# Index-add on one core: staged batches spread through the copies, their stores moved behind the last copy

## The chip, the cores and the metric

The kernel runs on one core of a Trainium2 chip. The metric is the device time of one execution in microseconds (us); the kernel before was run three times, with a median of 92.13 us. "The span" is the time from the first to the last of the program's own instructions in one profiled execution.

## The reference

For each of 32 batches, 128 rows of 256 float32 numbers are added to rows of a 512-row table. An index may occur several times in one batch, and then all of its rows are added.

```python
batch, seq, dim = 32, 512, 256
num_updates = 128
result = x.copy()
for b in range(batch):
    for i in range(num_updates):
        result[b, indices[b, i]] += source[b, i]
```

One batch of x, and so of the output, is 512 KB. One batch of source is 128 KB, and the sources of four batches are loaded together as one group of 512 KB.

## The kernel before, in words

Two ways lead to a finished batch.

**A direct batch** (0 to 25, `N_DIRECT = 26`). SP copies the whole batch from x to the output, DRAM to DRAM, in pieces of 4096 elements at most (`copy`, L97). GpSimd (POOL) gathers the 128 rows that the indices name into `got` with an indirect DMA (L189). TensorE multiplies a mask of equal indices (`same`) with the source rows, so that each row of the result holds the sum over all updates with that index (L266), and VectorE (DVE) adds this to the gathered rows, two batches at a time (L278). Then POOL scatters the rows over the copy with another indirect DMA (L346). A row whose index occurred earlier in the batch gets a place outside the table (`to_i`, L250) and isn't written. A scatter may start only when the copy of its batch has landed, since it overwrites rows of it, and when its sum is ready.

**A staged batch** (26 to 31). SP loads the whole batch into SBUF (`load_x`, L110). VectorE makes a one-hot matrix of the indices (L287), TensorE spreads the source rows over the 512 rows with it in two halves (L302), VectorE adds the halves to the loaded batch (L312), and ACT stores the finished batch (L323). There is no gather and no scatter.

**The order of the work.** Each engine runs its instructions in the order in which they are written.

- SP issues the index load, then source groups 0 and 1, then rounds of one source group, one load of a staged batch and two copies, with the source groups in the order 6, 7, 2, 3, 4, 5. After six rounds copies 10 to 25 remain and are issued one after the other. All this goes through one queue, which the profile calls q1. [...]
- ACT issues the six stores of the staged batches, each as soon as VectorE has finished the batch. They go through a queue of their own, q10.
- POOL issues 26 gathers, then 26 scatters in the order of the batches, then runs one `drain` (L354). Its transfers go through q0.
- TensorE and VectorE take the groups of four batches in order: for each group the mask of the next one (TensorE L206, VectorE L221, L233, L241, L250), then the sums of this one, then one staged batch.
- At the end SP waits for all six stores and then for all 26 scatters (L357), and the engines meet at the end of the program (L92). `tile_critical(no_gpsimd_drain=True)` is in both kernels, so the drain of L354 is the only one written.

Of the kernel before, what the change touches and what calls it, by code (L numbers as in the profile page):

```python
# [7 lines left out]
P = 128  # L8


GB = 4
COPY_DESC = 4096
N_DIRECT = 26


@with_exitstack
def kernel(
# [11 lines left out]
    nc = tc.nc  # L29

    B, S, D = x.shape
    _, NU = indices.shape
    CH = S // P
    assert NU == P and S % P == 0 and B % GB == 0 and N_DIRECT % 2 == 0
    NG = B // GB
    NGD = (N_DIRECT + GB - 1) // GB
    STAGED = list(range(N_DIRECT, B))

    f32 = mybir.dt.float32
    i32 = mybir.dt.int32  # L40
# [3 lines left out]
    x_rows = x.rearrange("b s d -> (b s) d")  # L44
    out_rows = out.rearrange("b s d -> (b s) d")

    sb = ctx.enter_context(tc.tile_pool(name="sb", bufs=1))
# [12 lines left out]
    row_i = sb.tile([P, B], i32)  # L60
    dup = sb.tile([P, B], f32)
    to_i = sb.tile([P, B], i32)
    src = [sb.tile([P, GB, D], f32, name=f"src{g}") for g in range(NG)]
    got = [sb.tile([P, 2, D], f32, name=f"got{h}") for h in range(N_DIRECT // 2)]
    same = [sb.tile([P, GB, P], f32, name=f"same{g}") for g in range(NGD)]
    earlier = [sb.tile([P, GB, P], f32, name=f"earlier{k}") for k in range(2)]
    staged = {b: sb.tile([P, CH, D], f32, name=f"staged{b}") for b in STAGED}
    onehot = {b: sb.tile([P, CH, P], f32, name=f"onehot{b}") for b in STAGED}
    N_ADD, N_SP = 3, 2
    idx_ps = pp.tile([P, B], f32, space=PSUM)  # L70
    bc = [pp.tile([P, GB, P], f32, space=PSUM, name=f"bc{k}") for k in range(2)]
    add = [pp.tile([P, 2, D], f32, space=PSUM, name=f"add{k}") for k in range(N_ADD)]
# [1 line left out]

    s_idx = tc.alloc_semaphore("s_idx")
    s_src = [tc.alloc_semaphore(f"s_src{g}") for g in range(NG)]
    s_copy = [tc.alloc_semaphore(f"s_copy{b}") for b in range(N_DIRECT)]
    s_got = [tc.alloc_semaphore(f"s_got{b}") for b in range(N_DIRECT)]
    s_in = {b: tc.alloc_semaphore(f"s_in{b}") for b in STAGED}
    s_out = tc.alloc_semaphore("s_out")  # L80
    s_store = tc.alloc_semaphore("s_store")
    sems = {n: tc.alloc_semaphore(f"s_{n}") for n in ("pool", "dve", "pe")}
    done = dict.fromkeys(sems, 0)

    def mark(name, ins):
        ins.then_inc(sems[name], 1)
        done[name] += 1
        return done[name]

    V, T, G, A = nc.vector, nc.tensor, nc.gpsimd, nc.scalar  # L90

    with tc.tile_critical(no_gpsimd_drain=True):  # L92

# [2 lines left out]
        def copy(b):  # L96
            nc.sync.dma_start(  # L97
                out=out[b].rearrange("(p c) d -> p (c d)", p=P),
                in_=x[b].rearrange("(p c) d -> p (c d)", p=P),
                max_dma_last_dim=COPY_DESC,  # L100
            ).then_inc(s_copy[b], 16)

        def load_src(g):
            nc.sync.dma_start(  # L104
                out=src[g][:, :, :],
                in_=source[g * GB : (g + 1) * GB].rearrange("e u d -> u e d"),
            ).then_inc(s_src[g], 16)

        def load_x(b):
            nc.sync.dma_start(  # L110
                out=staged[b][:, :, :], in_=x[b].rearrange("(j c) d -> j c d", c=CH)
            ).then_inc(s_in[b], 16)

        load_src(0)
        load_src(1)
        copies, sources, loads = list(range(N_DIRECT)), list(range(2, NG)), list(STAGED)
        sources = sources[-2:] + sources[:-2]
        while copies or sources or loads:
            if sources:
                load_src(sources.pop(0))  # L120
            if loads:
                load_x(loads.pop(0))
            for b in copies[:2]:
                copy(copies.pop(0))


        m = mark("pool", G.memset(ident[:, :], 0.0))  # L127
# [4 lines left out]
                out=ident[:, :], in_=ident[:, :], compare_op=Alu.not_equal, fill=1.0,  # L132
# [10 lines left out]
                out=place[:, :, :], pattern=[[1, CH], [CH, P]], base=0, channel_multiplier=0  # L143
# [8 lines left out]
                out=before[:, :, :], in_=before[:, :, :], compare_op=Alu.is_gt, fill=0.0,  # L152
# [8 lines left out]
        k = mark(  # L161
            "dve",
            V.tensor_copy(  # L163
                out=idx_bt[:, :],
                in_=idx_raw[:, :].rearrange("b (u w) -> b u w", w=2)[:, :, 0],
            ),
        )
        T.wait_ge(sems["pool"], k_const)
        T.wait_ge(sems["dve"], k)
        k = mark("pe", T.transpose(out=idx_ps[:, :], in_=idx_bt[:, :], identity=ident[:, :]))  # L170
        V.wait_ge(sems["pe"], k)
        k_rows = mark(
            "dve",
            V.tensor_tensor(out=row_i[:, :], in0=idx_ps[:, :], in1=base_f[:, :], op=Alu.add),
        )
# [7 lines left out]
        m = mark("dve", V.tensor_copy(out=place_f[:, :, :], in_=place[:, :, :]))  # L183
        V.wait_ge(sems["dve"], m)


        G.wait_ge(sems["dve"], k_rows)
        for b in range(N_DIRECT):
            G.indirect_dma_start(  # L189
                out=got[b // 2][:, b % 2, :],  # L190
                out_offset=None,
                in_=x_rows,
                in_offset=bass.IndirectOffsetOnAxis(ap=row_i[:, b : b + 1], axis=0),
            ).then_inc(s_got[b], 16)

        k_bc, k_same, k_to, k_sum, k_hot, k_spread = {}, {}, {}, {}, {}, {}

        def pe_broadcast(g):

            if g >= 2:  # L200
                T.wait_ge(sems["dve"], k_same[g - 2])
            for e in range(GB):
                b = g * GB + e
                k_bc[g] = mark(
                    "pe",
                    T.matmul(  # L206
                        out=bc[g % 2][:, e, :],
                        lhsT=ident[:, b : b + 1].to_broadcast([B, P]),
                        rhs=idx_bt[:, :],
                        start=True,  # L210
                        stop=True,
                    ),
                )
# [42 lines left out]
        def sums(g):  # L256

            T.wait_ge(s_src[g], 16)
            T.wait_ge(sems["dve"], k_same[g])
            for b in range(g * GB, min((g + 1) * GB, N_DIRECT)):  # L260
                h = b // 2
                if b % 2 == 0 and h >= N_ADD:
                    T.wait_ge(sems["dve"], k_sum[h - N_ADD])
                k = mark(
                    "pe",
                    T.matmul(  # L266
                        out=add[h % N_ADD][:, b % 2, :], lhsT=same[g][:, b % GB, :],
                        rhs=src[g][:, b % GB, :], start=True, stop=True,
                    ),
                )  # L270
                if b % 2 == 0:
                    continue
                V.wait_ge(sems["pe"], k)
                V.wait_ge(s_got[b - 1], 16)
                V.wait_ge(s_got[b], 16)
                k_sum[h] = mark(
                    "dve",
                    V.tensor_tensor(  # L278
                        out=got[h][:, :, :], in0=got[h][:, :, :],
                        in1=add[h % N_ADD][:, :, :], op=Alu.add,  # L280
                    ),
                )

        def dve_onehot(b):
            k_hot[b] = mark(
                "dve",
                V.tensor_scalar(  # L287
                    out=onehot[b][:, :, :], in0=place_f[:, :, :],
                    scalar1=idx_f[:, b : b + 1], scalar2=None, op0=Alu.is_equal,
                ),  # L290
            )
# [26 lines left out]
        def staged_batch(b):  # L318
            dve_onehot(b)
            pe_spread(b, 0)  # L320
            k = pe_spread(b, 1)
            A.wait_ge(sems["dve"], k)
            A.dma_start(  # L323
                out=out[b].rearrange("(j c) d -> j c d", c=CH), in_=staged[b][:, :, :]
            ).then_inc(s_store, 16)

        pe_broadcast(0)
        dve_masks(0)
        pe_broadcast(1)
        todo = list(STAGED)  # L330
        for g in range(NGD):
            if g + 1 < NGD:
                dve_masks(g + 1)
            if g + 2 < NGD:
                pe_broadcast(g + 2)
            sums(g)
            if todo:
                staged_batch(todo.pop(0))
        for b in todo:
            staged_batch(b)  # L340


        for b in range(N_DIRECT):
            G.wait_ge(s_copy[b], 16)
            G.wait_ge(sems["dve"], max(k_sum[b // 2], k_to[b // GB]))  # L345
            G.indirect_dma_start(  # L346
                out=out_rows,
                out_offset=bass.IndirectOffsetOnAxis(ap=to_i[:, b : b + 1], axis=0),
                in_=got[b // 2][:, b % 2, :],
                in_offset=None,  # L350
                bounds_check=B * S - 1,
                oob_is_err=False,
            ).then_inc(s_out, 16)
        G.drain()  # L354

        nc.sync.wait_ge(s_store, 16 * len(STAGED))
        nc.sync.wait_ge(s_out, 16 * N_DIRECT)  # L357
# [30 lines left out]
```

## Time and profile before

| what | value |
|---|---|
| three runs, median (lowest to highest) | 92.13 us (90.91 to 94.13) |
| the profiled execution's own time | 91.28 us |
| its span | 89.6 us |
| PE, DVE and POOL busy | 42.9, 36.2 and 53.6 us |
| bytes moved by the DMA engines | 30.61 MB |
| HBM read and written | 24.41 and 20.19 MB |

The page gives the span in 40 equal slices; a digit is the busy share of a slice in tenths. The DMA row is the mean over the core's 16 DMA engines, and the GB/s row is what they moved. A DRAM-to-DRAM copy counts once in GB/s but is read from HBM and written to it. A view of windows gives the same figures for any stretch of the span; there the share can pass 1, because transfers on one engine overlap a little. Times in the views are us from the start of the span.

### The profile page before, as it was taken

The page shows a single profiled execution, that of the slowest core. Times are in us where ns is not written, and L with a number is a line of the kernel's source. Part 1 is how long each engine was busy: PE and PEld are TensorE (multiplying, and loading weights), DVE is VectorE, ACT ScalarE, POOL GpSimd, SP SyncE. Part 2 cuts the span into 40 slices and gives each one's busy share as a digit, 9 for nine tenths or more (in the row PEclk, how much of TensorE's full clock was granted, in tenths as well). Part 3 has the DMA queues.
Part 4 walks back from the last instruction along what each step waited for, and adds up shares of the span by engine and source line. Part 5 has one row for each costly group of instructions (what it writes and reads, how often), then busy time and mean ns, then how long its engine had stood idle before and what let it go on. Part 6 is the DMA issues. An engine that isn't in the chain of part 4 may idle for free.

```text
span 89.6 us, 646 instructions
## 1 busy us (share of the span) xinstructions
PE 42.9 (48%) x157; PEld 32.8 (37%) x157; DVE 36.2 (40%) x65; POOL 53.6 (60%) x62
## 2 busy tenths in 40 slices
PE   0699950999299292949965358693000000000000
PEld 0698710776286271727745144581000000000000
DVE  2659416069669668342694964335000000000000
POOL 5778777877778777877786400446643448575400
PEclk9999999579999999555999985569655555555555
DMA  0899999999999999999999999999999999983200
GB/s 8 268 284 336 404 399 412 411 412 400 405 417 400 409 412 414 412 405 402 405 394 419 416 414 422 351 346 299 406 415 378 280 345 392 397 352 139 86 0 0
DMA packets 12243, 30.61 MB, mean 342 GB/s; under 512 B 1584, under 2 KB 5721, under 8 KB 12240
## 3 DMA queue, kind: packets, MB, share of 16 engines
q1 hardware_dynamic: 8880, 21.01, 63.2%
q0 software_dynamic: 2496, 6.42, 18.7%
q10 hardware_dynamic: 864, 3.15, 8.8%
q8 instruction: 1, 0.02, 0.1%
q14 instruction: 2, 0.02, 0.0%
HBM read 24.41 MB, written 20.19 MB: 498 GB/s over the span
## 4 chain that ended last, share of the span: by engine, by line
SPq 55%; DMA 24%; issue 8%; POOL 4%; POOLq 2%
DMA out_dram<-in_x_dram 24%; SPq L97 21%; SPq L104 17%; SPq L110 17%; POOL out_dram L346 4%; POOLq L354 1%; SPq L94 0%; POOLq L345 0%; POOLq L346 0%; SPq L383 0%; SPq L92 0%
## 5 line engine op out<-in xcount | busy, mean ns | idle before, releaser
L346 POOL DMA_INDIRECT out_dram<-got,to_i x26 | 26.0, 1000 | 21.1 <-DMA out_dram<-in_x_dram 7.8
L189 POOL DMA_INDIRECT got<-in_x_dram,row_i x26 | 25.3, 972 | 8.1 <-issue 7.0
L302 PE MATMUL spread<-src,onehot 128*128 128x256 f32 x48 | 16.4, 501 | 11.1 <-issue 7.5
L266 PE MATMUL add<-src,same 128*128 128x256 f32 x52 | 17.1, 484 | 4.1 <-DMA src<-in_source_dram 4.1
L302 PEld LDWEIGHTS spread<-src,onehot 128*128 128x128 f32 x48 | 11.9, 260 | 16.3 <-issue 14.2
L266 PEld LDWEIGHTS add<-src,same 128*128 128x128 f32 x52 | 11.7, 235 | 7.3 <-DMA src<-in_source_dram 4.7
L312 DVE TENSOR_TENSOR staged<-staged,spread 128x512 f32<-128x512 f32 x12 | 8.3, 688 | 13.1 <-PE spread L302 13.1
L278 DVE TENSOR_TENSOR got<-got,add 128x512 f32<-128x512 f32 x13 | 8.7, 685 | 8.4 <-PE add L266 4.5
L206 PE MATMUL bc<-idx_bt,ident 32*128 32x128 f32 x56 | 10.1, 342 | 0.0
L206 PEld LDWEIGHTS bc<-idx_bt,ident 32*128 32x128 f32 x56 | 9.1, 246 | 1.4 <-issue 0.7
L221 DVE TENSOR_TENSOR same<-bc,idx_f 128x512 f32<-128x512 f32 x7 | 4.8, 684 | 1.1 <-PE bc L206 1.1
L233 DVE TENSOR_TENSOR earlier<-same,before 128x512 f32<-128x512 f32 x7 | 4.8, 692 | 0.3
L241 DVE TENSOR_REDUCE dup<-earlier 128x4 f32<-128x512 f32 x7 | 4.8, 686 | 0.2
L287 DVE TENSOR_SCALAR onehot<-place_f,idx_f 128x512 f32<-128x512 f32 x6 | 2.9, 479 | 0.0
L170 PE MATMUL idx_ps<-ident,idx_bt 32*128 32x32 f32 x1 | 0.3, 279 | 3.1 <-DVE idx_bt L163 3.1
L159 DVE CAST base_f<-base 128x32 f32<-128x32 int32 x1 | 1.0, 993 | 1.7 <-POOL base L137 1.7
L170 PEld LDWEIGHTS idx_ps<-ident,idx_bt 32*128 32x128 f32 x1 | 0.2, 178 | 3.1 <-POOL before L147 3.1
L250 DVE SCALAR_TENSOR_TENSOR to_i<-dup,row_f 128x4 int32<-128x4 f32 x7 | 1.1, 162 | 0.2
L151 POOL TENSOR_SCALAR_AFFINE_SELECT before<-before 128x512 f32<-128x512 f32 x1 | 0.7, 708 | 0.1
L142 POOL IOTA place<- 128x512 int32 x1 | 0.6, 553 | 0.0
L147 POOL MEMSET before<- 128x512 f32 x1 | 0.5, 514 | 0.0
L127 POOL MEMSET ident<- 32x32 f32 x1 | 0.1, 114 | 0.5 <-SPq L92 0.5
(11 smaller groups left out, 2.0 us busy)
## 6 DMA issues: line engine op xcount, KB each, us to landing
out_dram<-in_x_dram SPq DMA_DIRECT2D x26, 512.0 KB, 17.9
src<-in_source_dram SPq DMA_DIRECT2D x8, 512.0 KB, 12.9
staged<-in_x_dram SPq DMA_DIRECT2D x6, 512.0 KB, 15.7
out_dram<-staged ACTq DMA_DIRECT2D x6, 512.0 KB
got<-in_x_dram,row_i POOLq DMA_INDIRECT x26, 5.9
out_dram<-got,to_i POOLq DMA_INDIRECT x26, 6.3
idx_raw<-in_indices_dram SPq DMA_DIRECT2D x1, 32.0 KB, 1.7
```

The source lines that it names most:

```text
L97: nc.sync.dma_start(out=out[b].rearrange("(p c) d -> p (c d)", p=P), in_=x[b].rearrange("(p c) d -> p (c d)", p=P), max_dma_last_dim=COPY_ ...
L104: nc.sync.dma_start(out=src[g][:, :, :], in_=source[g * GB : (g + 1) * GB].rearrange("e u d -> u e d"),).then_inc(s_src[g], 16)
L110: nc.sync.dma_start(out=staged[b][:, :, :], in_=x[b].rearrange("(j c) d -> j c d", c=CH)).then_inc(s_in[b], 16)
L189: G.indirect_dma_start(out=got[b // 2][:, b % 2, :], out_offset=None, in_=x_rows, in_offset=bass.IndirectOffsetOnAxis(ap=row_i[:, b : b + ...
L206: T.matmul(out=bc[g % 2][:, e, :], lhsT=ident[:, b : b + 1].to_broadcast([B, P]), rhs=idx_bt[:, :], start=True, stop=True,),
L221: V.tensor_tensor(out=same[g][:, :, :], in0=bc[g % 2][:, :, :], in1=idx_f[:, gs].unsqueeze(2).to_broadcast([P, GB, P]), op=Alu.is_equal,),
L233: V.tensor_tensor(out=earlier[g % 2][:, :, :], in0=same[g][:, :, :], in1=before[:, :, :], op=Alu.mult,),
L266: T.matmul(out=add[h % N_ADD][:, b % 2, :], lhsT=same[g][:, b % GB, :], rhs=src[g][:, b % GB, :], start=True, stop=True,),
L278: V.tensor_tensor(out=got[h][:, :, :], in0=got[h][:, :, :], in1=add[h % N_ADD][:, :, :], op=Alu.add,),
L302: T.matmul(out=spread[n % N_SP][:, c, :], lhsT=onehot[b][:, 2 * half + c, :], rhs=src[b // GB][:, b % GB, :], start=True, stop=True,),
L312: V.tensor_tensor(out=rows, in0=rows, in1=spread[n % N_SP][:, :, :], op=Alu.add),
L346: G.indirect_dma_start(out=out_rows, out_offset=bass.IndirectOffsetOnAxis(ap=to_i[:, b : b + 1], axis=0), in_=got[b // 2][:, b % 2, :], in ...
```

## The change

Three things change; what is computed doesn't.

- **Which batches are staged.** Six batches are staged as before, but now 7, 11, 15, 19, 23 and 27 in place of 26 to 31. Twenty-six are direct, as before; the direct batches are paired in their own order for `got` and for the sums, so that batch 6 shares a pair with batch 8.
- **The order of SP's queue.** Source groups are issued in the order 0 to 7, each two groups ahead, and each staged load two copies after its group. The six stores are no longer ACT's. SP issues them behind the last copy, each behind a wait for VectorE's last addition to that batch.
- **The order on VectorE and TensorE.** The staged batch of a group is computed behind the sums of the next group. A mask is made for the eighth group too, since batches 28 to 31 are direct now.

The gathers, the scatters and the drain keep their code and their number; their batch numbers follow the list of direct batches.

```diff
-N_DIRECT = 26
+STAGED = (7, 11, 15, 19, 23, 27)
...
-        copies, sources, loads = list(range(N_DIRECT)), list(range(2, NG)), list(STAGED)
-        sources = sources[-2:] + sources[:-2]
-        while copies or sources or loads:
-            if sources:
-                load_src(sources.pop(0))
-            if loads:
-                load_x(loads.pop(0))
-            for b in copies[:2]:
-                copy(copies.pop(0))
+        for g in range(NG):
+            if g + 2 < NG:
+                load_src(g + 2)
+            for b in range(g * GB, (g + 1) * GB):
+                if b in DIRECT:
+                    copy(b)
+                if b % GB == 1 and g * GB - 1 in STAGED:
+                    load_x(g * GB - 1)
...
-            A.wait_ge(sems["dve"], k)
-            A.dma_start(
-                out=out[b].rearrange("(j c) d -> j c d", c=CH), in_=staged[b][:, :, :]
-            ).then_inc(s_store, 16)
+            k_staged[b] = k
...
-        for g in range(NGD):
-            if g + 1 < NGD:
+        for g in range(NG):
+            if g + 1 < NG:
                 dve_masks(g + 1)
-            if g + 2 < NGD:
+            if g + 2 < NG:
                 pe_broadcast(g + 2)
             sums(g)
-            if todo:
-                staged_batch(todo.pop(0))
-        for b in todo:
-            staged_batch(b)
+            if g * GB - 1 in STAGED:
+                staged_batch(g * GB - 1)
...
         G.drain()
+
+
+        for b in STAGED:
+            nc.sync.wait_ge(sems["dve"], k_staged[b])
+            nc.sync.dma_start(
+                out=out[b].rearrange("(j c) d -> j c d", c=CH), in_=staged[b][:, :, :]
+            ).then_inc(s_store, 16)
```

SP's queue near its end, before. `src5` is a source group, `staged31` the load of a staged batch, and `out` from `x` a copy; x16 stands for sixteen of them in a row.

```order
L97 DMA out_0_dram<-in_x_dram 128x1024 x2
L104 DMA src4_78<-in_source_dram 128x4x256
L110 DMA staged30_108<-in_x_dram 128x1024
L97 DMA out_0_dram<-in_x_dram 128x1024 x2
L104 DMA src5_79<-in_source_dram 128x4x256
L110 DMA staged31_109<-in_x_dram 128x1024
L97 DMA out_0_dram<-in_x_dram 128x1024 x16
```

The same place now:

```order
L111 DMA staged19_108<-in_x_dram 128x1024
L98 DMA out_0_dram<-in_x_dram 128x1024 x3
L111 DMA staged23_109<-in_x_dram 128x1024
L98 DMA out_0_dram<-in_x_dram 128x1024 x3
L111 DMA staged27_110<-in_x_dram 128x1024
L98 DMA out_0_dram<-in_x_dram 128x1024 x2
L363 DMA out_0_dram<-staged7_105 128x1024
L363 DMA out_0_dram<-staged11_106 128x1024
L363 DMA out_0_dram<-staged15_107 128x1024
L363 DMA out_0_dram<-staged19_108 128x1024
L363 DMA out_0_dram<-staged23_109 128x1024
L363 DMA out_0_dram<-staged27_110 128x1024
```

The sixteen copies in a row have become runs of at most four, with loads between them, and the last rows of the queue are now the six stores; before, the last row was a copy.

VectorE's order around a staged batch late in the program, before:

```order
L250 SCALAR_TENSOR_TENSOR to_i_73<-dup_72,row_f_70 128x4
L278 TENSOR_TENSOR got10_92<-got10_92,add1_120 128x512
L278 TENSOR_TENSOR got11_93<-got11_93,add2_121 128x512
L287 TENSOR_SCALAR onehot31_115<-place_f_67,idx_f_68 128x512
L312 TENSOR_TENSOR staged31_109<-staged31_109,spread0_122 128x512
L312 TENSOR_TENSOR staged31_109<-staged31_109,spread1_123 128x512
L278 TENSOR_TENSOR got12_94<-got12_94,add0_119 128x512
```

And now:

```order
L272 TENSOR_TENSOR got9_91<-got9_91,add0_120 128x512
L272 TENSOR_TENSOR got10_92<-got10_92,add1_121 128x512
L281 TENSOR_SCALAR onehot23_115<-place_f_67,idx_f_68 128x512
L306 TENSOR_TENSOR staged23_109<-staged23_109,spread0_123 128x512
L306 TENSOR_TENSOR staged23_109<-staged23_109,spread1_124 128x512
L272 TENSOR_TENSOR got11_93<-got11_93,add2_122 128x512
L272 TENSOR_TENSOR got12_94<-got12_94,add0_120 128x512
L281 TENSOR_SCALAR onehot27_116<-place_f_67,idx_f_68 128x512
L306 TENSOR_TENSOR staged27_110<-staged27_110,spread0_123 128x512
L306 TENSOR_TENSOR staged27_110<-staged27_110,spread1_124 128x512
```

The last sums of direct batches (`got11`, `got12`) stand behind the update of batch 23 now, and the last thing that VectorE does is the update of batch 27, for which SP's last store waits.

More of the change, by code (lines that the diff above doesn't have):

```diff
@@ L33 @@
     CH = S // P
-    assert NU == P and S % P == 0 and B % GB == 0 and N_DIRECT % 2 == 0
+    assert NU == P and S % P == 0 and B % GB == 0
     NG = B // GB
-    NGD = (N_DIRECT + GB - 1) // GB
-    STAGED = list(range(N_DIRECT, B))
+    DIRECT = [b for b in range(B) if b not in STAGED]
+    N_DIRECT = len(DIRECT)
+    assert N_DIRECT % 2 == 0
     f32 = mybir.dt.float32
@@ L64 @@
     got = [sb.tile([P, 2, D], f32, name=f"got{h}") for h in range(N_DIRECT // 2)]
-    same = [sb.tile([P, GB, P], f32, name=f"same{g}") for g in range(NGD)]
+    same = [sb.tile([P, GB, P], f32, name=f"same{g}") for g in range(NG)]
     earlier = [sb.tile([P, GB, P], f32, name=f"earlier{k}") for k in range(2)]
@@ L76 @@
     s_src = [tc.alloc_semaphore(f"s_src{g}") for g in range(NG)]
-    s_copy = [tc.alloc_semaphore(f"s_copy{b}") for b in range(N_DIRECT)]
-    s_got = [tc.alloc_semaphore(f"s_got{b}") for b in range(N_DIRECT)]
+    s_copy = {b: tc.alloc_semaphore(f"s_copy{b}") for b in DIRECT}
+    s_got = {b: tc.alloc_semaphore(f"s_got{b}") for b in DIRECT}
     s_in = {b: tc.alloc_semaphore(f"s_in{b}") for b in STAGED}
@@ L88, in mark @@
         return done[name]
-    V, T, G, A = nc.vector, nc.tensor, nc.gpsimd, nc.scalar
+    V, T, G = nc.vector, nc.tensor, nc.gpsimd
     with tc.tile_critical(no_gpsimd_drain=True):
@@ L184 @@
         V.wait_ge(sems["dve"], m)
[L187 to L194, printed above, removed]
         k_bc, k_same, k_to, k_sum, k_hot, k_spread = {}, {}, {}, {}, {}, {}
+        k_staged = {}
         def pe_broadcast(g):
@@ L259, in sums @@
             T.wait_ge(sems["dve"], k_same[g])
-            for b in range(g * GB, min((g + 1) * GB, N_DIRECT)):
-                h = b // 2
-                if b % 2 == 0 and h >= N_ADD:
+            for b in range(g * GB, (g + 1) * GB):
+                if b in STAGED:
+                    continue
+                n = DIRECT.index(b)
+                h = n // 2
+                if n % 2 == 0 and h >= N_ADD:
                     T.wait_ge(sems["dve"], k_sum[h - N_ADD])
@@ L266, in sums @@
                     T.matmul(
-                        out=add[h % N_ADD][:, b % 2, :], lhsT=same[g][:, b % GB, :],
+                        out=add[h % N_ADD][:, n % 2, :], lhsT=same[g][:, b % GB, :],
                         rhs=src[g][:, b % GB, :], start=True, stop=True,
@@ L270, in sums @@
                 )
-                if b % 2 == 0:
+                if n % 2 == 0:
                     continue
                 V.wait_ge(sems["pe"], k)
-                V.wait_ge(s_got[b - 1], 16)
+                V.wait_ge(s_got[DIRECT[n - 1]], 16)
                 V.wait_ge(s_got[b], 16)
@@ L329, with gather, scatter @@
         pe_broadcast(1)
-        todo = list(STAGED)
-        for g in range(NGD):
-            if g + 1 < NGD:
+        for g in range(NG):
+            if g + 1 < NG:
                 dve_masks(g + 1)
-            if g + 2 < NGD:
+            if g + 2 < NG:
                 pe_broadcast(g + 2)
             sums(g)
-            if todo:
-                staged_batch(todo.pop(0))
-        for b in todo:
-            staged_batch(b)
-        for b in range(N_DIRECT):
+            if g * GB - 1 in STAGED:
+                staged_batch(g * GB - 1)
+        def gather(n):
+            b = DIRECT[n]
+            G.indirect_dma_start(
+                out=got[n // 2][:, n % 2, :],
+                out_offset=None,
+                in_=x_rows,
+                in_offset=bass.IndirectOffsetOnAxis(ap=row_i[:, b : b + 1], axis=0),
+            ).then_inc(s_got[b], 16)
+        def scatter(n):
+            b = DIRECT[n]
             G.wait_ge(s_copy[b], 16)
-            G.wait_ge(sems["dve"], max(k_sum[b // 2], k_to[b // GB]))
+            G.wait_ge(sems["dve"], max(k_sum[n // 2], k_to[b // GB]))
             G.indirect_dma_start(
@@ L348 @@
                 out_offset=bass.IndirectOffsetOnAxis(ap=to_i[:, b : b + 1], axis=0),
-                in_=got[b // 2][:, b % 2, :],
+                in_=got[n // 2][:, n % 2, :],
                 in_offset=None,
@@ L353 @@
             ).then_inc(s_out, 16)
-        G.drain()
+        G.wait_ge(sems["dve"], k_rows)
+        for n in range(N_DIRECT):
+            gather(n)
+        for n in range(N_DIRECT):
+            scatter(n)
+        G.drain()
+        for b in STAGED:
[3 more added lines that the diff above has]
+            ).then_inc(s_store, 16)
         nc.sync.wait_ge(s_store, 16 * len(STAGED))
```

## The prediction

> **What bounds the kernel now.** I read the page's slices first, then its queues, and then the last ten microseconds row by row.
>
> ```profile
> DMA  0899999999999999999999999999999999983200
> q1 hardware_dynamic: 8880, 21.01, 63.2%
> q0 software_dynamic: 2496, 6.42, 18.7%
> q10 hardware_dynamic: 864, 3.15, 8.8%
> ```
>
> The DMA engines are full from the second slice to the 35th, and no compute engine is over 60% busy. The three queues' packets take 63.2 + 18.7 + 8.8 = 90.7% of 16 engines for 89.6 us, which is 81.3 us. So the kernel is bound by moving bytes, and only time in which the engines are not full, or move slowly, can be won. The view of windows shows where that is (the last two columns are the DMA share and GB/s):
>
> ```profile
> 2.50:10.00 7.50, 6.89 (x28) 6.47 (x29) 5.61 (x14) 5.76 (x7) 1.00 0.96 318
> 10.00:40.00 30.00, 20.22 (x79) 14.79 (x78) 17.37 (x31) 22.68 (x25) 0.88 1.04 408
> 40.00:54.00 14.00, 9.86 (x37) 7.52 (x38) 8.78 (x16) 7.94 (x8) 0.87 1.04 410
> 56.00:63.00 7.00, 4.38 (x12) 3.30 (x12) 2.74 (x5) 3.81 (x4) 0.72 1.02 334
> 63.00:67.00 4.00, 0.00 (x0) 0.00 (x0) 0.00 (x0) 2.10 (x3) 0.54 1.03 416
> 67.00:73.00 6.00, 0.00 (x0) 0.00 (x0) 0.00 (x0) 2.75 (x3) 0.50 1.04 331
> 73.00:79.00 6.00, 0.00 (x0) 0.00 (x0) 0.00 (x0) 3.54 (x5) 0.50 1.02 392
> 79.00:82.00 3.00, 0.00 (x0) 0.00 (x0) 0.00 (x0) 2.39 (x3) 0.50 0.69 267
> 82.00:85.30 3.30, 0.00 (x0) 0.00 (x0) 0.00 (x0) 1.17 (x2) 0.50 0.20 72
> 85.30:89.60 4.30, 0.00 (x0) 0.00 (x0) 0.00 (x0) 0.00 (x0) 0.50 0.00 0
> ```
>
> Three losses stand here. From 79 to 85.3 the engines run empty. From 56 to 63 and 67 to 73 they are full but move 331 to 334 GB/s in place of 410. And the last 4.3 us move nothing.
>
> What are the engines waiting for at the end? POOL's timeline, with its idle time and releaser in brackets:
>
> ```profile
> 78.62 0.98 POOL L346 DMA_INDIRECT out_dram<-got,to_i  x1 [0.78 <-DMA out_dram<-in_x_dram]
> 79.91 0.99 POOL L346 DMA_INDIRECT out_dram<-got,to_i  x1 [0.30 <-issue]
> 81.20 0.99 POOL L346 DMA_INDIRECT out_dram<-got,to_i  x1 [0.30 <-issue]
> 82.87 0.99 POOL L346 DMA_INDIRECT out_dram<-got,to_i  x1 [0.69 <-issue]
> ```
>
> The scatters are paced by the copies that they overwrite: the 23rd waits for its copy, and the last one is late by another 0.39 us over a back-to-back pair, so its copy too has only just landed, at about 82. Nothing stands behind the last copy in any queue but scatters. The final wait and the drain close the program:
>
> ```profile
> L354 POOLq DRAIN  x1: 5530/5530/5530, 82.7 to 82.7; - x1
> L357 SPq EVENT_SEMAPHORE  x1: 17/17/17, 85.2 to 85.2; - x1
> L92 SPq EVENT_SEMAPHORE  x3: 17/28/28, 85.5 to 85.7; - x3
> SPq L92 <- POOLq L92: 2.5, 1, 2.5
> ```
>
> The last scatter lands at 85.2, SP is through its own meeting at 85.7, and then it waits 2.5 us for POOL, whose drain lasts until 82.7 + 5.5 = 88.2. After that 1.4 us remain to 89.6.
>
> **Term 1, the empty tail.** The same bytes move in the same kinds of transfers: 26 copies, 26 gathers, 26 scatters, 8 sources, 6 loads, 6 stores. What moves is the place of 3.15 MB of stores. They take 8.8% of 89.6, or 7.9 us of all 16 engines, and in the new order they follow the last copy in q1. So when the last copy lands, some 8 us of work remains in which the last scatters can land, where there was nothing. The tail's empty time is (1.04 - 0.69) x 3 + (1.04 - 0.20) x 3.3 = 1.05 + 2.77 = 3.8 engine-us, or 3.7 us at a share of 1.04. I keep the first 1.0 of it as lost: there the copies were still landing, and the engines ended unevenly, which stores may do as well. **Term 1 is -2.7 us; bounds -3.7 (no unevenness) to 0.**
>
> This needs the store of the last staged batch to be issued in time. Behind the load of batch 27 come the update, SP's wait and the store.
>
> ```profile
> L302 PE MATMUL spread<-src,onehot 128*128 128x256 f32 x48 | 16.4, 501 | 11.1 <-issue 7.5
> L312 DVE TENSOR_TENSOR staged<-staged,spread 128x512 f32<-128x512 f32 x12 | 8.3, 688 | 13.1 <-PE spread L302 13.1
> ```
>
> With the spread done ahead of the load, the two additions take 1.4 us; with none of it done, four matmuls at 0.5 and the additions take 3.4 us. Behind the load in q1 stand two copies and five stores, 7 x 0.52 MB, which at 410 GB/s is 8.9 us. So the update is hidden with over 5 us to spare; without that cover it would cost 3.4 us plus the landing of a store.
>
> **What costs nothing.** The mask of the eighth group adds 2.2 us to VectorE and 1.4 us to TensorE:
>
> ```profile
> L221 DVE TENSOR_TENSOR same<-bc,idx_f 128x512 f32<-128x512 f32 x7 | 4.8, 684 | 1.1 <-PE bc L206 1.1
> L206 PE MATMUL bc<-idx_bt,ident 32*128 32x128 f32 x56 | 10.1, 342 | 0.0
> POOL out_dram L346 <- DVE onehot L287: 5.9, 2, 5.2
> ```
>
> That is three passes of 0.69 and a short one, and four matmuls of 0.34. Both engines are idle for over half of the span. On VectorE these and the staged updates now stand ahead of later sums: the sums of batches 24 to 26 are behind the load of 19, and those of 28 to 31 behind the load of 23. Scatters may wait there for 3 to 4 us, as one does now (5.2 us, the third row) while the DMA engines stay full. The load of 23 stands three copies ahead of copy 28 in q1, so the last four sums are ready before their copies. Without this cover the last scatters start late, which the 8 us of stores absorb first. SP pays for the six stores' issue in place of ACT, behind the last copy, where SP has nothing else to do:
>
> ```profile
> 58.02 6.80 SPq L97 DMA_DIRECT2D out_dram<-in_x_dram  x2
> out_dram<-in_x_dram SPq DMA_DIRECT2D x26, 512.0 KB, 17.9
> ```
>
> SP is done with the last copy at 64.8 and has 17 us until it lands, so six issues fit in.
>
> **Term 2, the slow stretches.** At 410 GB/s the bytes of 56 to 63 would have taken 5.7 us, those of 67 to 73 4.8, those of 73 to 79 5.7: 1.3 + 1.2 + 0.3 = 2.8 us are lost. SP's last load and ACT's last two staged stores were issued here:
>
> ```profile
> 38.14 2.31 SPq L110 DMA_DIRECT2D staged<-in_x_dram  x1
> 50.72 0.34 ACTq L323 DMA_DIRECT2D out_dram<-staged  x1
> 61.05 0.34 ACTq L323 DMA_DIRECT2D out_dram<-staged  x1
> ```
>
> The loads have landed long before 56, and after it nearly only copies and a few scatters move, but for these stores. Soon after the second store the rate is back at 416 for four microseconds (63 to 67). Where loads, gathers and stores run among the copies (10 to 54) it is 408 to 410. The new order puts a load behind every two or three copies to the end, but takes the stores out. Bounds: -2.8 if all of it goes, +2.8 if it doubles. The mixed rows are nearer to the new order than the pure ones, but the stores are missing: **I take a third, -0.9 us.**
>
> [...]
>
> **Term 3, the drain.** With Terms 1 and 2 the last byte lands at 85.2 - 2.7 - 0.9 = 81.6, and SP is ready at 82.1. The last copy lands (7.9 + 0.6) / 1.04 = 8.2 us before the last byte, at 73.4 (0.6 is for two scatters: 18.7% of 89.6 over 52 indirect transfers is 0.32 each), and POOL reaches the drain about a microsecond later.
>
> ```profile
> DMA to landing us min/median/max: 2.4/6.3/7.8
> ```
>
> That is the scatters' time from issue to landing. One execution doesn't tell what the drain waits for. If it takes 5.5 us from its start, it ends at 80 and is hidden: -2.5. If it ends 3.0 us behind the last scatter's landing (88.2 - 85.2), that scatter lands at 74.4 + 6.3 = 80.7, the drain ends at 83.7, and SP still waits 1.6: -0.9. Nothing decides between them. **I take the middle, -1.7.**
>
> **Sum.** -2.7 - 0.9 - 1.7 = -5.3: the span goes from 89.6 to 84.3, and the profiled execution's 91.28 to 86.0. The median of the three runs lies 0.85 above that execution, so the predicted time is **86.8 us**.
>
> **Rivals.**
>
> *Copies slow each other down (slower).* If the copies' slow rate is due to what is near them, removing the stores can spread it. The page's slices show how low it goes:
>
> ```profile
> GB/s 8 268 284 336 404 399 412 411 412 400 405 417 400 409 412 414 412 405 402 405 394 419 416 414 422 351 346 299 406 415 378 280 345 392 397 352 139 86 0 0
> ```
>
> From 40 to the last copy are 33 us. At 332 GB/s throughout, 33 x (1 - 332/410) = 6.3 are lost, 3.5 more than now, and the sum is -2.7 + 3.5 - 1.7 = -0.9: 91.2. At 290, near the two worst slices (299, 280), 9.7 are lost, the sum is +2.5, and the time is 94.6. The point from which the change loses is where 7.2 us are lost, 321 GB/s. For it: the slow stretches lie where the stores pause. Against: 40 to 54 is mixed much as the new middle, at 410. Chances 8% for about 332, 6% for under 321.
>
> *The last scatter still ends it.* The change then doesn't do what it says: the copies don't get ahead by what the stores gave up, because scatters take the room. If it lands at 80.5 instead of 73.4, the last scatter, its landing and the drain follow as now, 1.5 us sooner than now, with the stores beside them: 89.8, at the median 90.6. For it: the scatters' backlog of now (5.2 us of waiting) becomes traffic beside the copies. Against: it is the same traffic, only earlier. Chance 12%.
>
> *The stores wait for the update of batch 27.* If its load lands late on a slow DMA engine and the 5 us of slack go, the last store ends 3 us later: 89.8. Against it the slack above. Chance 6%.
>
> *Everything is won.* The terms at their lower bounds, -3.7 - 2.8 - 2.5 = -9.0, give 83.1. Chance 10% for under 85.
>
> **How the numbers follow.** The forecast has the remaining 58%. A difference of about 2% is what a measurement of this kernel can tell from none; that is 1.84 us, so faster means under 90.3. The forecast, the full gain and the late store lie there: 74%. The lasting tail and the copies at 332 lie within it: 20%. Slower: 6%. The range is 84.2 to 91.4; it leaves out about 8% below and 8% above. The forecast's own range is 85 to 89.5.
>
> **What would show each step.** Term 1: the DMA row stays at 9 to within one or two slices of its end, the last landing is a store's, and the last scatter is issued at 74 to 76. Term 2: the rate in 45 to 73 is near 395 GB/s, with no slices under 300. Term 3: SP's wait for POOL at the end is 0 to 1.6 us. The queue q10 is gone and q1 has 24.2 MB. The forecast is wrong if the last copy lands after 78, if the slices before it lie under 330 GB/s, or if POOL waits for VectorE in the last five scatters.

## The result, and the profile after

The changed kernel takes 85.15 us (median of 4 runs, 83.68 to 85.62); the kernel before, run beside it, 91.91 us (median of 4, 90.91 to 94.13). The ratio is 0.921, with a 95% interval of 0.899 to 0.942: about 8% faster. Some of these executions are over 1.5% longer than the quickest one of their kernel (94.13 beside 90.91, 85.37 and 85.62 beside 83.68); the ratio and its interval leave those out, the medians don't. The forecast was 86.8 us. The profiled execution took 84.92 us, its span is 83.2.

The page's slices and queues of the changed kernel first:

```profile
DMA  0799999999999999999999999999999999999810
GB/s 2 234 326 309 381 406 408 348 413 418 397 417 420 404 408 407 413 423 398 408 416 420 396 411 409 414 411 423 412 408 362 411 416 418 418 417 418 330 65 0
q1 hardware_dynamic: 9744, 24.15, 74.5%
q0 software_dynamic: 2496, 6.42, 19.7%
```

The queue q10 is gone, and its 3.15 MB are in q1. The DMA row is full up to the third slice from its end. In the GB/s row the long dip of before (422 351 346 299 406 415 378 280 345) is one slice of 362. The same in the view of windows:

```profile
10.00:40.00 30.00, 18.40 (x65) 13.38 (x63) 12.55 (x23) 22.68 (x25) 0.86 1.03 406
45.00:54.00 9.00, 5.21 (x25) 4.11 (x26) 5.75 (x10) 6.90 (x7) 0.99 1.04 409
54.00:62.00 8.00, 2.58 (x12) 1.92 (x11) 4.49 (x8) 4.93 (x5) 0.80 1.03 417
62.00:66.00 4.00, 3.33 (x9) 2.77 (x10) 1.25 (x3) 2.96 (x3) 0.55 1.02 377
66.00:73.00 7.00, 3.79 (x17) 2.70 (x15) 3.88 (x6) 3.95 (x5) 1.00 1.03 418
73.00:79.00 6.00, 0.00 (x0) 0.00 (x0) 0.00 (x0) 0.98 (x1) 0.74 0.96 389
79.00:81.15 2.15, 0.00 (x0) 0.00 (x0) 0.00 (x0) 0.00 (x0) 0.50 0.17 67
```

The last two columns again are the DMA share and GB/s. The last copies now run at 417 and 418 GB/s, where 331 to 334 stood. The tail isn't quite full: from 79 to 81.15, when the last byte lands, the share is 0.17.

POOL's timeline for the last four scatters, and the rows of the three lines that end the program:

```profile
68.54 0.98 POOL L344 DMA_INDIRECT out_dram<-got,to_i  x1 [1.24 <-DMA out_dram<-in_x_dram]
69.83 0.99 POOL L344 DMA_INDIRECT out_dram<-got,to_i  x1 [0.30 <-issue]
71.84 0.98 POOL L344 DMA_INDIRECT out_dram<-got,to_i  x1 [1.03 <-DVE staged L306]
73.37 0.98 POOL L344 DMA_INDIRECT out_dram<-got,to_i  x1 [0.55 <-issue]
```

```profile
L358 POOLq DRAIN  x1: 8676/8676/8676, 73.1 to 73.1; - x1
L368 SPq EVENT_SEMAPHORE  x1: 17/17/17, 79.7 to 79.7; - x1
L93 SPq EVENT_SEMAPHORE  x3: 17/17/28, 81.3 to 81.6; - x3
```

The last scatter is issued at 73.4 in place of 82.9 and has landed by 79.7, where SP is through its wait for the scatters (L368). SP's own waits, from the view of waits, show what comes after it:

```profile
SPq L363 <- DVE staged L306: 10.5, 3, 4.6
SPq L368 <- DMA out_dram<-got,to_i: 7.5, 1, 7.5
SPq L93 <- DMA out_dram<-staged: 1.5, 1, 1.5
SPq L93 <- POOLq L93: 0.3, 1, 0.3
```

The last thing to land is a store (1.5 us of waiting behind the scatters, until 81.15), and POOL's drain, done at 73.15 + 8.68 = 81.8, holds SP for 0.3 us in place of 2.5.

**Where the 6.4 us of span came from.** The last landing moves from 85.2 to 81.15, 4.1 us. The packets took 90.7% of 89.6 us before, 81.3 us of all 16 engines; now (74.5 + 19.7)% of 83.2 = 78.4. So 2.9 us came from faster packets, and the remaining 1.2 from a fuller tail. SP's wait for POOL gives another 2.2, and 4.1 + 2.2 = 6.3.

### The profile page after: what moved, and what is told of

Same layout as the page of the kernel before. It is cut to its first block, busy times and chain, and to the rows that moved or that the text cites. A ratio compares the mean times of both kernels' runs of the same rounds, so it can differ in the third digit from the quotient of the medians.

```text
span 83.2 us, 665 instructions
## 1 busy us (share of the span) xinstructions
PE 45.1 (54%) x165; PEld 34.9 (42%) x165; DVE 38.4 (46%) x69; POOL 53.4 (64%) x62
## 3 DMA queue, kind: packets, MB, share of 16 engines
q1 hardware_dynamic: 9744, 24.15, 74.5%
q0 software_dynamic: 2496, 6.42, 19.7%
## 4 chain that ended last, share of the span: by engine, by line
SPq 47%; DMA 19%; PE 9%; issue 6%; DVE 6%; POOLq 1%; POOL 1%; DVEq 0%
SPq L98 31%; DMA staged<-in_x_dram 19%; SPq L105 10%; PE spread L296 6%; SPq L111 6%; PE add L260 2%; DVE staged L306 2%; POOLq L358 1%; POOL out_dram L344 1%; DVE got L272 1%; DVE earlier L224 1%; DVE dup L232 1%; DVE same L212 1%; DVE onehot L281 0%; SPq L95 0%
## 5 line engine op out<-in xcount | busy, mean ns | idle before, releaser
L296 PE MATMUL spread<-src,onehot 128*128 128x256 f32 x48 | 15.0, 468 | 22.9 <-DVE onehot L281 17.7
L296 PEld LDWEIGHTS spread<-src,onehot 128*128 128x128 f32 x48 | 10.8, 236 | 27.1 <-issue 25.4
L260 PE MATMUL add<-src,same 128*128 128x256 f32 x52 | 17.7, 492 | 0.0
L197 PE MATMUL bc<-idx_bt,ident 32*128 32x128 f32 x64 | 13.4, 380 | 0.0
L197 PEld LDWEIGHTS bc<-idx_bt,ident 32*128 32x128 f32 x64 | 12.0, 281 | 2.6 <-issue 2.0
L212 DVE TENSOR_TENSOR same<-bc,idx_f 128x512 f32<-128x512 f32 x8 | 5.5, 683 | 1.1 <-PE bc L197 1.1
L224 DVE TENSOR_TENSOR earlier<-same,before 128x512 f32<-128x512 f32 x8 | 5.5, 692 | 0.3
L232 DVE TENSOR_REDUCE dup<-earlier 128x4 f32<-128x512 f32 x8 | 5.5, 686 | 0.3
```

The source lines that it names most:

```text
L197: T.matmul(out=bc[g % 2][:, e, :], lhsT=ident[:, b : b + 1].to_broadcast([B, P]), rhs=idx_bt[:, :], start=True, stop=True,),
L212: V.tensor_tensor(out=same[g][:, :, :], in0=bc[g % 2][:, :, :], in1=idx_f[:, gs].unsqueeze(2).to_broadcast([P, GB, P]), op=Alu.is_equal,),
L224: V.tensor_tensor(out=earlier[g % 2][:, :, :], in0=same[g][:, :, :], in1=before[:, :, :], op=Alu.mult,),
L232: V.tensor_reduce(out=dup[:, gs], in_=earlier[g % 2][:, :, :], op=Alu.max, axis=mybir.AxisListType.X,),
L260: T.matmul(out=add[h % N_ADD][:, n % 2, :], lhsT=same[g][:, b % GB, :], rhs=src[g][:, b % GB, :], start=True, stop=True,),
L296: T.matmul(out=spread[n % N_SP][:, c, :], lhsT=onehot[b][:, 2 * half + c, :], rhs=src[b // GB][:, b % GB, :], start=True, stop=True,),
```

## The experiments

The theory: copies run at full rate where loads stand among them to the end, the stores fill the tail behind the last copy, and the drain is then hidden. The rivals: one part alone brings it (the stores' place, or the spread loads), or the drain alone does. The series of e and f ran on one chip, those of g and h on a chip each, and each kernel is compared with the kernel before in the same series.

### Each half alone

e1 is the changed kernel with the stores back on ACT, each as soon as its batch is ready:

```diff
+            A.wait_ge(sems["dve"], k)
+            A.dma_start(
+                out=out[b].rearrange("(j c) d -> j c d", c=CH), in_=staged[b][:, :, :]
+            ).then_inc(s_store, 16)
-            k_staged[b] = k
```

> The changed kernel with one thing undone: ACT issues each staged store as soon as the batch is updated; which batches are staged and where their loads stand is left as changed. Theory (the stores behind the last copy cover the last scatters, and so also hide the drain): both go, 2.7 to 3.7 us of empty tail and 2.2 us of drain come back, the even rate of the copies stays: 89.5 to 90.5 us, with the last landing a scatter's and SP's wait for POOL at 2 us or more. Rival (the loads spread among the copies did it all, by taking away the slow stretches): 85 to 86.5 us.

e2 is the kernel before (26 to 31 staged) with only its stores moved to SP, behind the last copy.

> The kernel before with one thing changed: SP issues the six staged stores behind the last copy; batches 26 to 31 stay staged and their loads stay at the head of the queue. Theory: the empty tail and the drain are won, 4.9 us, but the copies now run for some 25 us with nothing but scatters among them, which costs 1 to 3 us more than the 2.8 of before: 87.5 to 90 us, with slices under 350 GB/s before the last copy lands. Rival (spread loads did it all): 91 to 92.5 us.

e1 took 98.98 us (98.01 to 99.48), e2 94.38 (93.41 to 95.31), the kernel before beside them 94.85 (93.44 to 96.82). No theory expected e1 to be slower, by a ratio of 1.047 (1.031 to 1.063); something else was at work, which the next series looks into. The two still tell one thing, the rate of their copies. The slices of e2, and two stretches of it:

```profile
GB/s 14 268 310 396 415 345 388 417 402 408 402 417 387 412 403 405 407 405 408 417 415 343 332 279 341 357 311 294 389 356 392 412 421 417 308 160 295 102 0 0
```

```profile
48.00:62.00 14.00, 9.62 (x41) 7.52 (x42) 8.12 (x14) 4.80 (x5) 0.80 1.04 327
62.00:72.00 10.00, 6.74 (x32) 5.05 (x31) 8.38 (x16) 5.69 (x7) 1.00 1.02 364
```

Here no store runs before the last copy, and the copies behind the loads move 327 GB/s with the engines full. So the stores near them were not what slowed the copies of before. The other half, loads spread and stores left on ACT, has this for the same stretch (f1, e1's repetition below):

```profile
50.00:70.00 20.00, 11.17 (x45) 8.33 (x46) 10.78 (x19) 4.38 (x5) 0.77 1.03 403
```

At the same DMA share, 403 GB/s with loads among the copies, 327 without. In that stretch f1 also had more scatters and some of its stores beside the copies. The closest pair has none of the stores and almost no scatters (0.03 MB each), f1 first, then e2:

```profile
52.00:60.00 8.00, 4.74 (x16) 3.58 (x16) 2.72 (x5) 1.97 (x2) 0.55 1.03 392
```

```profile
48.00:56.00 8.00, 5.32 (x20) 4.28 (x21) 3.61 (x6) 1.97 (x2) 0.65 1.04 318
```

392 with a load behind every two or three copies, 318 with copies alone. (The two copy different batches there; no run separates that.) A load isn't the only thing that keeps the rate up. The kernel before has no load after 54, and there 63 to 67, with a store and scatters beside the copies, runs at 416, and 74 to 79, with copies and scatters alone, at this rate:

```profile
74.00:79.00 5.00, 0.00 (x0) 0.00 (x0) 0.00 (x0) 3.33 (x4) 0.50 1.02 394
```

But 67 to 73 runs at 331 with as large a share of scatters. So what the rate depends on beyond "copies alone are slow" is not shown.

### Without the drain

e3 is the kernel before, e4 the changed kernel, each without `G.drain()`.

> The kernel before without its drain on GpSimd; all of the computation is kept, since SP waits for every scatter. If the drain sets the end, SP's wait of 2.5 us for POOL goes: 89.2 to 89.8 us. Rival (something else at the end of the program waits for the scatters' queue just as long, or the drain's time is only where a fixed end shows): 91.5 to 92.3 us.

> The changed kernel without its drain on GpSimd. Theory (the stores hide it but for 0.3 us): 84.5 to 85.3 us. Rival (the drain still costs its 2.5 us somewhere at the end): 82.5 to 83.2 us.

e3 took 96.30 us (94.74 to 97.47) and e4 103.95 (100.23 to 105.73), beside 94.85: nothing was won. e4 lies far from both of its expectations, for a reason that the next series shows. SP's waits of e3, and the rows of POOL's drains at its last line:

```profile
SPq L382 <- PEq L382: 5.0, 2, 4.2
```

```profile
L382 POOLq DRAIN  x3: 40/177/4312, 87.5 to 92.8; - x3
```

e3 still ends with a drain on POOL, though none is written: it takes 4.3 us, and it starts at 87.5, when the last scatter has landed (SP is through its wait at 87.2). The written drain of the kernel before, from 82.7 to 88.2, runs beside the last scatter's landing at 85.2 and leaves SP 2.5 us of waiting. The rival that the drain is a cost to be removed falls: from the last scatter's landing to the end of the span e3 takes 93.0 - 87.2 = 5.8 us, the kernel before 89.6 - 85.2 = 4.4.

### The changed kernel again, beside both halves

In that series the kernel before was itself 3 us slower than beside the result, and e1 and e4 slower still, so all but e4 were repeated (f1 is e1 again, f2 is e2, f3 is e3), with the changed kernel itself, f0, among them.

> The changed kernel itself, beside the next three on one chip, since the four runs before were on a chip where VectorE waited 23 us for gathers whose packets had long moved. Theory: 5 to 7.5 us less than the kernel before, with no such wait. Rival (the change is worth less where VectorE is held up): within 3 us of the kernel before, or slower, with the wait of 20 us and more in the trace.

> The changed kernel with the stores back on ACT, each issued as soon as its batch is updated; the second try of this edit. Theory: the empty tail and the drain come back, the even rate stays: 3.5 to 5.5 us over the changed kernel on the same chip, the last landing a scatter's, SP's wait for POOL 2 us or more. Rival (the loads spread among the copies did it all): within 1.5 us of the changed kernel.

> The kernel before with only its six stores moved behind the last copy on SP; the second try of this edit. Theory: 2 to 4 us less than the kernel before on the same chip (the tail and the drain are won, some of it is given back by slower copies, with slices under 350 GB/s). Rival (spread loads did it all): within 1 us of the kernel before.

> The kernel before without its drain; the second try of this edit. If the drain sets the end: 2 to 2.7 us less than the kernel before on the same chip, and SP's wait for POOL at the end is gone. Rival (another wait of POOL's takes its place): within 0.7 us of the kernel before, with SP still waiting over 1.5 us.

| kernel | median (lowest to highest), us |
|---|---|
| before, in this series | 95.62 (94.12 to 98.82) |
| f0, the changed kernel | 99.06 (96.54 to 101.17) |
| f1, its stores on ACT | 100.31 (98.87 to 102.89) |
| f2, only the stores moved | 94.98 (93.97 to 98.77) |
| f3, before without drain | 98.41 (96.78 to 99.86) |

The changed kernel, 8% faster in the result, is slower than the kernel before on this chip: by 3.4 us in the median and by 2.4 in the quickest run, with ranges that overlap. f0's DMA row, its longest wait of VectorE, and VectorE's timeline show what differs:

```profile
DMA  0899999999999999999999999999993441262610
```

```profile
DVE got L272 <- remote: 29.5, 2, 19.4
```

```profile
19.96 0.16 DVE L241 SCALAR_TENSOR_TENSOR to_i<-dup,row_f 128x4 int32<-128x4 f32 x1
39.55 0.69 DVE L272 TENSOR_TENSOR got<-got,add 128x512 f32<-128x512 f32 x1 [19.42 <-remote]
50.33 0.69 DVE L272 TENSOR_TENSOR got<-got,add 128x512 f32<-128x512 f32 x1 [10.09 <-remote]
```

VectorE waits 19.4 and 10.1 us for its two sums of the third group ("remote": no event in the profile shows what released it). In the result's trace the same two sums run at 20.15 and 21.64. The work behind them starts some 29 us late, the last scatters come at 90, and the tail is empty. All eight runs have such waits, of 24 to 33 us in sum (in e3, f2 and f3 a part of them stands under "issue"). So the times of these eight runs compare kernels under late signals and tell the worth of the parts only there: f2 is equal to before (ratio 0.999, 0.992 to 1.006), and f1, with its stores on ACT, is 1.25 us over f0 with ranges that overlap. f2's stores, moved behind the last copy, had to wait for the late VectorE too (SP waits 23.7 us for it in four waits of its trace), so equal times don't show that moving the stores alone is worth nothing without late signals.

### Which signal is late

The sum waits for two gathers and for TensorE, each of which counts up a semaphore when it is done; that count is the signal. First theory: the gathers' signals. g_before and g_changed leave out the addition of the gathered rows of x: VectorE adds source rows instead, into a buffer `upd` that is scattered, and waits for no gather.

```diff
-                V.wait_ge(s_got[DIRECT[n - 1]], 16)
-                V.wait_ge(s_got[b], 16)
...
-                        out=got[h][:, :, :], in0=got[h][:, :, :],
-                        in1=add[h % N_ADD][:, :, :], op=Alu.add,
+                        out=upd[h][:, :, :], in0=add[h % N_ADD][:, :, :],
+                        in1=src[g][:, 0:2, :], op=Alu.add,
```

> The kernel before, but VectorE waits for no gather: it adds source rows to the sums in place of the gathered rows, into a buffer of its own, which is scattered. All transfers stay in kind, number and order; what is left out is the addition of the gathered rows of x. Theory (on this chip it is the late gathers' signals that hold VectorE up, and the order of the queue does what it did in the prediction): no wait of VectorE over 6 us, 90.5 to 93 us. Rival (other signals are late too): VectorE waits over 10 us for something else, 94 us or more.

> The changed kernel with the same piece left out: VectorE waits for no gather. Theory: 84 to 86.5 us, 5 to 7.5 less than the kernel before with that piece left out, the last landing a store's, SP's wait for POOL under 1 us. Rival (other signals are late too, and the changed order leaves less time behind them): no less than the kernel before with that piece left out, 94 us or more, with VectorE waiting over 10 us for a staged load or a source.

On another chip, they took 97.08 us (95.35 to 98.83) and 100.41 (98.42 to 102.65), the kernel before 95.36 (92.26 to 96.87); so the rivals' times came, not the theories'. g_changed's timeline of VectorE, and of TensorE with the matmuls that these sums wait for:

```profile
39.68 0.69 DVE L271 TENSOR_TENSOR upd<-add,src 128x512 f32<-128x512 f32 x1 [20.38 <-remote]
50.46 0.69 DVE L271 TENSOR_TENSOR upd<-add,src 128x512 f32<-128x512 f32 x1 [10.09 <-remote]
```

```profile
16.32 1.56 PE L261 MATMUL add<-src,same 128*128 128x256 f32 x6
51.70 3.75 PE L295 MATMUL spread<-src,onehot 128*128 128x256 f32 x8 [33.81 <-DVE upd L271]
```

The theory falls: with no gather to wait for, VectorE waits just as long. Only TensorE's signal is left, and its matmuls were done at 17.9. The signal is late, not the work. The semaphore records in the traces agree: f0's matmuls of the first three groups end by 18.2, but between 17 and 53 us its trace has records of TensorE's signals only at 29.0, 33.9, 39.5, 45.8 and 50.3, and VectorE's two sums start with the third and the last of them. In the result's trace each of these signals is recorded within 0.1 us of the end of its matmul.

The ten traces with late signals have one more thing in common: they are short of records. The rows of the gathers on the pages of f0 and of the result:

```profile
got<-in_x_dram,row_i POOLq DMA_INDIRECT x26
```

```profile
got<-in_x_dram,row_i POOLq DMA_INDIRECT x26, 5.9
```

f0's row has no time to landing, because the records of it are missing. Each of these ten traces holds 547 to 617 records of landings, each of the other four 1578 to 1584. So late signals and lost records come together in these fourteen traces; what brings both about, no run tells.

### With fewer signals from TensorE

The next theory is a guess that none of the traces so far shows: that the delay is per signal, so that fewer signals come in time. Both kernels with one signal per mask, per pair of sums and per half of a spread, in place of one per matmul:

```diff
-                k = mark(
-                    "pe",
-                    T.matmul(
-                        out=add[h % N_ADD][:, n % 2, :], lhsT=same[g][:, b % GB, :],
-                        rhs=src[g][:, b % GB, :], start=True, stop=True,
-                    ),
+                mm = T.matmul(
+                    out=add[h % N_ADD][:, n % 2, :], lhsT=same[g][:, b % GB, :],
+                    rhs=src[g][:, b % GB, :], start=True, stop=True,
                 )
                 if n % 2 == 0:
                     continue
+                k = mark("pe", mm)
```

> The changed kernel with fewer signals from TensorE, and nothing else: one for each mask, each pair of sums and each half of a spread, where there was one for every product; the whole computation is kept. In the ten runs so far TensorE's signals came out one in 5 us between 16 and 50 us, although its products were issued, and VectorE waited for them. Theory (the delay is per signal, and with it gone the new order gives what it gave in the result): VectorE's waits there fall from 30 us to under 15, 84 to 90 us, and 3 us or more under the kernel before with the same edit. Rival (the delay lasts until about 50 us however few signals there are): VectorE's waits stay at 25 us or more, 96 us or more.

> The kernel before with the same edit. Theory: 90 to 93 us, a scatter landing last and SP waiting 2.5 us for POOL. Rival (the delay lasts however few signals there are): 94 us or more, as without the edit, and less than the changed kernel with the edit.

h_changed_few_signals took 86.0 us (84.65 to 87.72), h_before_few_signals 92.09 (91.49 to 95.45), the kernel before 91.77 (90.55 to 97.27). On this third chip the signals came in time, by both traces, and by its time in the kernel before too. So whether fewer signals cure the lateness stays untested; by themselves they win nothing (1.006, 1.002 to 1.011). What the pair does show is the change a second time, without late signals: 0.930 of the kernel before (0.923 to 0.938), 6.1 us under its own counterpart. The slices and queues of h_before_few_signals:

```profile
GB/s 13 276 291 381 403 383 406 408 406 385 407 417 396 390 414 414 408 399 401 397 412 406 415 425 350 346 332 311 419 373 363 295 350 361 391 372 145 91 0 0
q1 hardware_dynamic: 8880, 21.01, 63.6%
q0 software_dynamic: 2496, 6.42, 18.8%
q10 hardware_dynamic: 864, 3.15, 8.6%
```

And of h_changed_few_signals:

```profile
GB/s 5 220 321 323 394 409 386 276 411 412 404 415 411 394 401 410 423 413 405 411 414 414 410 406 409 407 422 362 415 413 402 384 403 412 426 420 402 216 42 0
q1 hardware_dynamic: 9744, 24.15, 73.7%
q0 software_dynamic: 2496, 6.42, 19.3%
```

The long dip of the one (350 346 332 311, then 373 363 295 350 361) is gone in the other. The packets take 91.0% of 90.3 = 82.2 us in the one and 93.0% of 84.8 = 78.9 in the other: 3.3 us from faster packets, as against 2.9 in the result. SP's waits at the end, before and changed:

```profile
SPq L92 <- POOLq L92: 2.5, 1, 2.5
```

```profile
SPq L93 <- DMA out_dram<-staged: 1.8, 1, 1.8
```

The wait of 2.5 us for POOL is gone here as well; the last wait that is left at this line is that for a store.

## Why the prediction was right, step by step

The time (85.15 for 86.8), the sign and the direction of all three terms were right. That the number came so close is partly luck: Term 1 was foretold 1.5 us too large and Term 2 2.0 too small, and the two errors mostly cancel.

- **The bound** (moving bytes; only empty or slow time of the DMA engines can be won): right. In both pairs nearly all of the gain is faster packets, a fuller tail and SP's last wait.
- **Term 2, the slow stretches: -0.9 foretold, -2.9 measured.** This is the step that was furthest off: "I take a third". Nearly all of it went; of the 2.8 us only about 4 x (1 - 377/410) = 0.3 are left, in 62 to 66. The prediction feared that the missing stores would cost rate. e2 shows that their absence alone doesn't bring the rate back, and the changed kernel, whose copies also have no stores beside them, runs at 417. The loads, gone from the last copies of before and spread to the end now, do bring it back: f1, with the loads spread and the stores on ACT, keeps 392 where copies alone have 318. That is shown for the rate, though not that loads alone can do it; how much of the time each half brings was measured only under late signals, and stays open without them.
- **Term 1, the empty tail: -2.7 foretold, -1.2 measured.** The stores do follow the last copy. Its landing is read from the last scatter's start, with POOL's time from a copy's landing to the scatter behind it, which the chain of waits of the kernel before shows:

```profile
51.31 21.91 DMA out_dram<-in_x_dram
...
74.00 0.41 POOL out_dram L346
```

  That copy landed at 51.31 + 21.91 = 73.22, the scatter began 0.78 later; so the changed kernel's last copy landed at 73.37 - 0.78 = 72.6, where 73.4 was foretold, and 8.5 us of work followed it, where 8.2 were foretold. But "I keep the first 1.0 of it as lost" was too little: 6 x (1.04 - 0.96) + 2.15 x (1.04 - 0.17) = 2.4 engine-us are empty before the last landing. The last store wasn't issued too late for it, although SP waited 4.6 us for VectorE ahead of each of the last two stores, the second time until the update of batch 27 at 71.8. The windows show the engines still full five microseconds after that issue, and then emptying step by step:

```profile
77.00:77.50 0.50, 0.00 (x0) 0.00 (x0) 0.00 (x0) 0.00 (x0) 0.50 1.05 422
78.00:78.50 0.50, 0.00 (x0) 0.00 (x0) 0.00 (x0) 0.00 (x0) 0.50 0.75 305
79.00:79.50 0.50, 0.00 (x0) 0.00 (x0) 0.00 (x0) 0.00 (x0) 0.50 0.33 131
80.00:80.50 0.50, 0.00 (x0) 0.00 (x0) 0.00 (x0) 0.00 (x0) 0.50 0.14 57
```

  So it is the engines ending unevenly, which the prediction named and priced too low.
- **Term 3, the drain: -1.7 foretold, -2.2 measured.** Hidden but for 0.3 us. Neither reading of it was right. From the end of the last scatter's instruction to the end of the drain it took 82.65 + 5.53 - 83.86 = 4.3 us in the kernel before, and 81.82 - 74.35 = 7.5 in the changed one. The second reading, 3.0 us behind the scatter's landing, measured 81.8 - 79.7 = 2.1. Both kernels fit a drain that ends 4.3 us behind the end of the last scatter's instruction or 2.2 behind its landing, whichever is later, and so does h_changed_few_signals, where the scatter landed at 81.2 and the drain ended at 83.4. No run tests that rule.
- **What costs nothing:** right in the result, and the text named the cover, VectorE idle for over half of the span. Three of its readings were wrong without harm. The group counts give 48 / 6 = 8 matmuls for a staged batch and 56 / 7 = 8 for a mask, not four: the mask of the eighth group costs TensorE 8 x 0.34 = 2.7 us, not 1.4, and an update with none of the spread done would take 8 x 0.5 + 1.4 = 5.4 us, which is all of the slack. The update of batch 27 took 2.3 us, from the load's landing at 69.5 to 71.8, since the spread had begun before the landing. And only copy 26, not three copies, stands between the load of 23 and copy 28 in q1. The eight runs with late signals took the cover away and show what that can cost: f0, whose masks and staged updates stand ahead of later sums, takes 4.1 us more than f2 in the median and 2.6 in the quickest run; f2 keeps the old order. That the order is the reason was argued from POOL's waits for sums, not isolated.
- **The rivals.** The copies didn't slow each other down, and the last scatter doesn't end it. The sign that the forecast was to be wrong by, a wait of POOL for VectorE in the last five scatters, is in the timeline (71.84, 1.03 us, "DVE staged"), but it is a coincidence of two events: no scatter waits for that update in the program's order, and 71.84 less 0.78 is 71.06, which is when the trace has the copy of that batch landed.
- **A stretch that was passed over.** The prediction counts three losses, but the first row of its windows, 318 GB/s from 2.5 to 10 at a share of 0.96, where the first sources are loaded beside copies, lies as low as the stretches of copies, and it counts nothing there. The changed kernel starts no faster, with 320 at a share of 0.97 over the same stretch; no run shows why.

## What to carry to other kernels

Copies from DRAM to DRAM that are queued in one long row run some 20% slower here (318 to 334 GB/s) than with loads among them (392 in f1, 406 to 418 in the changed kernel from 10 us on, but for 377 from 62 to 66), so deal the loads out to the very end instead of issuing them early. Put transfers that nothing waits for (stores of finished buffers) behind those that something waits for (copies that a scatter must overwrite), so that the dependent chain ends beside them (here the last scatter landed at 79.7 in place of 85.2). And a change that leans on an idle engine as cover is only as good as that cover: the same kernel that won 8% was 2.4 to 3.4 us slower than before where signals to that engine came late.

## What the runs showed of the hardware that was not expected

- **Copies alone are slow with full engines**: 318 GB/s at a DMA share of 1.04 with nothing beside them (e2, 48 to 56), against 392 with loads among them (f1, 52 to 60) and 406 to 418 with loads and with gathers or scatters (the changed kernel, 10 to 40, 54 to 62 and 66 to 73). Copies with scatters alone ran at 331 in one stretch and 394 in another (the kernel before, 67 to 73 and 74 to 79); why is open.
- **A drain on POOL behind an indirect DMA** ended 4.3 us behind the end of the last scatter's instruction in the kernel before, and 7.5 us behind it in the changed one, where that scatter's data landed beside stores (at 79.7, the instruction having ended at 74.35). Without it, in e3, the program's closing drain takes 4.31 us, all of it behind the last landing.
- **TensorE's signals came late in ten of the fourteen traces**, all of those of e, f and g: VectorE was held 24 to 33 us by sums whose matmuls were done at 18 to 25 us, on two of the three chips of the experiments. The kernel before took 95 us there in place of 92, the changed one 99 in place of 85. All ten of these traces lack about two thirds of the landing records. The cause is open: fewer signals and other chips were tried, but not together on a chip that shows it.
